# Scanned states by group, slot and part: a change of layout in a two-layer encoder trunk

## The chip, the core and the metric

The kernel runs on one core of one Trainium2 chip. A core has five engines that run their own instruction streams and meet at semaphores: TensorE (PE, with its weight loads PEld), VectorE (DVE), ScalarE (ACT), GpSimd (POOL) and SyncE (SP), which mostly issues transfers (DMA). On-chip memory is SBUF, with 128 partitions, and PSUM, which PE writes. The metric is the time of one execution on the device, in microseconds (us), lower being better.

## The reference

The program is a trunk of two layers over 256 tokens of width 2048. Layer 0 is attention, and the change does not touch it. Layer 1 is a state-space layer: the input projection gives u and a gate z; u is cut into 128 groups of 16 channels, and every group drives 64 complex states in two directions of time.

```python
    bu_re = jnp.einsum('sbgc,gpc->sbgp', u, bb_re)
    bu_im = jnp.einsum('sbgc,gpc->sbgp', u, bb_im)
    ...
    _, _, s_re, s_im = lax.associative_scan(_ssm_combine, (a_re, a_im, bu_re, bu_im), reverse=reverse, axis=0)
    return jnp.einsum('gcp,sbgp->sbgc', c_re, s_re) - jnp.einsum('gcp,sbgp->sbgc', c_im, s_im)
```

In words: the state at each token is the state of the token before, multiplied by a complex number per group and state, plus an input; the output is the real part of a product with c. Forward and backward outputs are summed, a skip and a GELU follow, then a GLU product with a 2048 x 2048 matrix, the gate silu(z), the output projection, a residual sum and a layer norm.

## The kernel before

**Weights.** All large products are made in three passes of rounded operands. A weight chunk of 512 KB is loaded by SP (`raw`, L157, four buffers), rounded on ACT (`wh`, L146, 1024 elements a partition), and its rest is formed on DVE or POOL (`wl`, L148; in the input projection of layer 1 nearly always on POOL). PE then uses both (L210 to L212). Each engine takes its instructions in the order in which the program was built: the kernel's own step loop weaves small tasks of several lanes ("in", "scan", "out", "g", "glu") between the weight chunks, and a wait of one instruction holds up all that stands behind it on its engine.

**The state-space part.** Tokens are taken in chunks of L = 4, so a sequence has NCH = 64 chunks, called slots here. The 128 groups are handled in 16 pieces of PG = 8 groups, and the states of eight pieces (64 groups) are held in one tile V. Partition p of V is a state: 0 to 63 forward, 64 to 127 backward. Along the free axis V holds, per slot, a real and an imaginary part for 64 groups: 64 x 2 x 64 numbers of 4 bytes a partition.

- `in_products` (lane "in"): PE makes the inputs of all slots for one piece (L879) in two PSUM banks `vps`; ACT copies each bank into V (L883), 512 numbers a partition.
- `scan_task` (lane "scan"): 62 steps for each half of 64 groups, all on DVE. A step multiplies the state of slot c - 1 by the coefficients (L896: both products at once into `scp`, which lies in PSUM as the coefficients `cf` do), and adds the two products to slot c (L897 and L898).
- `out_task` (lane "out"): for each piece the scanned states are copied into `su`, ordered by part, group and slot (L918 for the forward partitions, always on ACT; L919 for the backward ones, on ACT for the first eight pieces and on DVE for the last eight, slots in falling order). PE then makes the outputs of the piece (`yps`, L947) from `su`, `om` and `up`, ACT applies GELU (`yg`, L952) and sends the result to HBM, from where `g_task` loads it again and splits it into `gT` (L244 on ACT, L245 on DVE). PSUM has three banks for `vps` and `yps`, so the outputs of a piece must wait until ACT has read those of the third piece before it.

The input projection of the gate (`z`, L1049 and L1051) runs on PE while scan and outputs are under way; the GLU product over `gT` follows, then the output projection.

The coefficient tile is made once, far ahead (L383 to L386), and copied into PSUM when the scan's buffers are opened (L994 and L995).

Of the kernel before, what the change touches and what calls it, by code (L numbers as in the profile page):

```python
# [9 lines left out]
F32 = mybir.dt.float32  # L10
# [3 lines left out]
ALU = mybir.AluOpType  # L14
# [10 lines left out]
G = 128  # L25
# [3 lines left out]
NCH = S // L  # L29
# [3 lines left out]
PG = 8  # L33
# [7 lines left out]
class Trunk:  # L41
# [3 lines left out]
    def __init__(self, ctx, tc, a):  # L45
# [3 lines left out]
        self.s0, self.s1 = self.pool("s0"), self.pool("s1")  # L49
        P = lambda name, bufs, space: ctx.enter_context(tc.tile_pool(name=name, bufs=bufs, space=space))  # L50
        self.dr = P("dr", 1, DRAM)
        self.held, self.tops = ExitStack(), ExitStack()
# [231 lines left out]
    def ssm_tables(self, tp, pp):  # L284

        nc, a, v = self.nc, self.a, self.nc.vector
# [20 lines left out]
        n = T("ex_n")  # L307
# [12 lines left out]
        pw = [None] + [(pws[0][:, k], pws[1][:, k]) for k in range(4)]  # L320
# [48 lines left out]
        f, b = slice(0, 64), slice(64, 128)  # L369
# [10 lines left out]
                            nc.gpsimd.tensor_copy(self.op[i][f, :, c, :, k], src[f])  # L380
                            nc.gpsimd.tensor_copy(self.op[i][b, :, c, :, 3 - k], src[b])

        self.coef = self.const.tile([128, 2, 2, G], F32, name="coef")  # L383
        nc.gpsimd.tensor_copy(self.coef[:, 0], pw[4][0].unsqueeze(1).to_broadcast([128, 2, G]))
        nc.gpsimd.tensor_copy(self.coef[:, 1, 0], pw[4][1])
        v.tensor_scalar(self.coef[:, 1, 1], pw[4][1], -1.0, None, ALU.mult)  # L386

    def ssm_scratch(self):
        d = self.dr
# [476 lines left out]

    def in_products(self, pc, im, up):
        if pc == 8:
            self.V.append(self.s1.tile([128, NCH, 2, 64], F32, tag="s1", name="V"))
        nc, V, g0 = self.nc, self.V[pc // 8], pc % 8 * PG  # L870

        pss = [self.bank("vps").rearrange("p (g r s) -> p g r s", g=4, r=2) for _ in range(2)]
        with self.urgent() if self.IN_URG else ExitStack(), ExitStack() as order:
            for pr in range(4):
                for ri in range(2):
                    for hf, d in ((0, 0), (1, 1), (0, 1), (1, 0)):
                        h = slice(hf * 64, hf * 64 + 64)
                        mv = up[h, 1, pr] if d == 0 else up[h, 0, pr, ::-1]
                        m = nc.tensor.matmul(pss[hf][d * 64:d * 64 + 64, pr, ri], lhsT=im[h, pr, ri, d * 64:d * 64 + 64], rhs=mv, start=True, stop=True)  # L879
                        order.enter_context(self.tc.issue_after(m.ins))  # L880
        with self.urgent():
            for hf in range(2):
                nc.scalar.copy(V[:, :, :, g0 + hf:g0 + PG:2].rearrange("p s r g -> p g r s"), pss[hf])  # L883
        self.flags.add(("V", pc))

    def scan_task(self, p0, p1):

        v = self.nc.vector
        n, g0 = (p1 - p0) * PG, p0 % 8 * PG
        V = self.V[p0 // 8][:, :, :, g0:g0 + n]  # L890
        cf = self.coef[:, :, :, p0 * PG:p1 * PG]
        shp = [128, 2, 2, n]
        for c in range(1, NCH - 1):
            P = self.sc.tile([128, 512], F32, tag="scp", name="scp")[:, :4 * n].rearrange("q (e r g) -> q e r g", e=2, r=2)
            with self.urgent():
                v.tensor_tensor(P, cf, V[:, c - 1].unsqueeze(1).to_broadcast(shp), ALU.mult)  # L896
                v.tensor_tensor(V[:, c], V[:, c], P[:, 0], ALU.add)  # L897
                self.swept = v.tensor_tensor(V[:, c], V[:, c], P[:, 1, ::-1], ALU.add).ins  # L898
            yield
        t = self.now + self.OUT_LAG[p1 == NPIECE]  # L900
        while self.now < t:
            yield
        if p1 == NPIECE:
            self.lanes["out"]["width"] = self.OUT_W2
        for pc in range(p0, p1):
            self.add("out", self.out_task(pc))

    def out_task(self, pc):

        nc, v, wk = self.nc, self.nc.vector, self.wk1  # L910
        b, q = pc // 4, pc % 4
        V = self.V[pc // 8]
        gs = slice(pc % 8 * PG, pc % 8 * PG + PG)
        su = wk.tile([128, 2, PG, NCH], F32, tag="q4", name="su", bufs=self.Q4)
        f, r = slice(0, 64), slice(64, 128)
        nc.gpsimd.memset(su[f, :, :, 0:1], 0.0)
        nc.gpsimd.memset(su[r, :, :, NCH - 1:], 0.0)
        nc.scalar.copy(su[f, :, :, 1:], V[f, 0:NCH - 1, :, gs].rearrange("p s r g -> p r g s"))  # L918
        (v.tensor_copy if pc >= 8 else nc.scalar.copy)(su[r, :, :, :NCH - 1], V[r, NCH - 2::-1, :, gs].rearrange("p s r g -> p r g s"))  # L919
        self.flags.add(("su", pc))  # L920
        tag, bufs = ("im", self.NIM) if self.n_in == NPIECE and self.OMT else ("q4", self.Q4)
        om = wk.tile([128, 2, PG, C * L], F32, tag=tag, name="om", bufs=bufs)
        nc.sync.dma_start(om, self.OMd[pc])
        if pc == 0:
            self.tt = {0: self.turned(0, self.toeplitz(0))}
        if q == 1 and b < NB - 1:
            self.tr = self.toeplitz(b + 1)
        if q == 3 and b < NB - 1:
            self.tt[b + 1] = self.turned(b + 1, self.tr)
        tt = self.tt[b]  # L930
        up = wk.tile([128, 4, NCH], F32, tag="up", name="up2", bufs=3)
        nc.sync.dma_start(up, self.Ud[pc].rearrange("h c t a k -> (h c t) a k"))
        yield
        yield
        ps = self.pm.tile([128, 512], F32, tag="pm", name="yps", bufs=self.npm)

        h = [slice(g % 2 * 64, g % 2 * 64 + 64) for g in range(PG)]
        o = [ps[h[g], g // 2 * NCH:g // 2 * NCH + NCH] for g in range(PG)]
        even, odd = range(0, PG, 2), range(1, PG, 2)
        jobs = [(g, None) for g in even] + [(g, ri) for ri in range(2) for g in range(PG)] + [(g, None) for g in odd]  # L940
        seen = set()
        with ExitStack() as order:
            for n, (g, ri) in enumerate(jobs):
                lhsT = tt[q // 2][h[g], q % 2 * 4 + g // 2].rearrange("q e t -> q (e t)") if ri is None else om[:, ri, g]
                rhs = up[h[g], g // 2] if ri is None else su[:, ri, g]
                stop = ri is None if g % 2 else ri == 1
                m = nc.tensor.matmul(o[g], lhsT=lhsT, rhs=rhs, start=g % 2 not in seen, stop=stop, skip_group_check=True)  # L947
                seen.add(g % 2)
                order.enter_context(self.tc.issue_after(m.ins))
        yield  # L950
        yg = wk.tile([128, 4, NCH], F32, tag="yg", name="yg", bufs=2)
        nc.scalar.activation(yg.rearrange("p a k -> p (a k)"), ps[:, :S], AF.Gelu_apprx_tanh)  # L952
        nc.scalar.dma_start(self.Gd[pc].rearrange("(a h) c t k -> (h c t) a k", h=2), yg)
        self.add("g", self.g_task(pc), *[("su", p) for p in range(8)])
# [32 lines left out]
    def open(self, ssm):  # L987

        self.until(lambda: self.idle("prep"))
        self.prep.close()  # L990
        self.s2 = self.pool("s2", side="right")
        wk = self.wk1 = self.pool("wk1", ssm, side="right")
        self.psum(*self.PSB)
        cf = self.sc.tile([128, 2, 2, G], F32, name="cf")  # L994
        self.nc.scalar.copy(cf, self.coef)  # L995
        self.coef = cf
        self.V = [self.s2.tile([128, NCH, 2, 64], F32, tag="s2", name="V")]
        p0 = 0
        for p1 in self.BATCH:
            self.add("scan", self.scan_task(p0, p1), *[("V", p) for p in range(p0, p1)])  # L1000
            p0 = p1
        self.flags.add("open")
# [207 lines left out]
```

## Time and profile before

| | us |
|---|---|
| median of 3 runs | 894.93 |
| lowest and highest of them | 891.43, 897.63 |
| the profiled execution's own time | 895.47 |
| span of that execution in the trace | 893.7 |

| engine | busy, us | share of the span |
|---|---|---|
| PE | 836.7 | 94% |
| DVE | 654.6 | 73% |
| ACT | 513.9 | 58% |
| POOL | 262.2 | 29% |

The trace covers one execution. Busy time counts instructions of an engine between their start and end; a matmul that runs at a lower granted clock counts as busy for longer, so a busy PE is not a PE at its peak. The share of an engine is a mean over stages: which engine ends a wait has to be read from the stretch in question. Most of layer 1's state-space work lies between 440 and 710 us.

### The profile page before, as it was taken

How to read it: one execution, taken by the hardware profiler on the slowest of the kernel's cores; microseconds unless marked ns; L12 is line 12 of the kernel's file. 1: busy time of each engine (PE TensorE's matmuls, PEld its weight loads, DVE VectorE, ACT ScalarE, POOL GpSimd, SP SyncE). 2: the span in 40 equal slices, each digit the busy share in tenths (PEclk: the TensorE clock that was granted, in tenths of full speed). 3: DMA queues.
4: the chain of work that ended last, by engine and by line, in shares of the span. 5: the costliest groups of instructions: out<-in, count | busy, mean ns of one | idle time of the engine just before them, and what ended most of it. 6: DMA issues, size and time to landing. Idle time of an engine off the chain costs nothing.

```text
span 893.7 us, 18431 instructions
## 1 busy us (share of the span) xinstructions
PE 836.7 (94%) x7244; PEld 759.5 (85%) x7244; DVE 654.6 (73%) x1178; ACT 513.9 (58%) x738; POOL 262.2 (29%) x182
## 2 busy tenths in 40 slices
PE   6999999999999989997999999988997999999992
PEld 4788989889899877886899998987996999988882
DVE  3999889999979968888400598899932459856646
ACT  3554456868677574453565666489749547443321
POOL 0008600000002323333766665843783100000004
PEclk9999999999999999999999999998998899999997
DMA  9765587777676676896789898783996966876723
GB/s 240 237 193 182 140 244 256 208 198 238 166 228 161 199 201 198 244 300 219 254 259 281 252 288 247 224 223 110 276 296 222 269 197 206 237 235 221 241 81 94
DMA packets 217798, 195.82 MB, mean 219 GB/s; under 512 B 67648, under 2 KB 174064, under 8 KB 217456
## 3 DMA queue, kind: packets, MB, share of 16 engines
q1 hardware_dynamic: 200688, 189.93, 71.1%
q10 hardware_dynamic: 17024, 4.72, 2.3%
q8 instruction: 57, 0.93, 0.5%
q14 instruction: 29, 0.24, 0.1%
HBM read 168.39 MB, written 26.21 MB: 218 GB/s over the span
## 4 chain that ended last, share of the span: by engine, by line
PE 62%; DMA 14%; DVE 9%; ACT 5%; issue 5%; SPq 3%; POOL 1%; ACTq 0%; DVEq 0%; POOLq 0%
PE acc L184 10%; PE acc L185 10%; PE acc L186 10%; PE acc L210 8%; PE acc L211 8%; PE acc L212 8%; DMA Ud<-ut 5%; PE yps L947 2%; DMA up<-Ud 1%; PE kps L460 1%; SPq L496 1%; PE vps L879 1%; ACT su L918 1%; DMA raw<-in_w_in_ssm_dram 1%; DMA Gd<-yg 1%
## 5 line engine op out<-in xcount | busy, mean ns | idle before, releaser
L146 ACT CAST wh<-raw 128x1024 fp32r<-128x1024 f32 x234 | 245.1, 1050 | 232.5 <-PE acc L186 76.4
L148 POOL TENSOR_TENSOR wl<-raw,wh 128x1024 fp32r<-128x1024 f32 x84 | 205.9, 2458 | 361.1 <-ACT wh L146 330.9
L148 DVE TENSOR_TENSOR wl<-raw,wh 128x1024 fp32r<-128x1024 f32 x150 | 188.2, 1258 | 49.0 <-ACT wh L146 48.6
L210 PE MATMUL acc<-h1T,wh 128*128 128x256 f32 x512 | 147.2, 292 | 1.9 <-ACT ut L849 1.4
L211 PE MATMUL acc<-h1T,wh 128*128 128x256 f32 x512 | 145.7, 286 | 0.0
L212 PE MATMUL acc<-h1T,wl 128*128 128x256 f32 x512 | 145.0, 284 | 0.0
L896 DVE TENSOR_TENSOR scp<-cf,V 128x256 f32<-128x256 f32 x124 | 53.6, 433 | 72.0 <-ACT V L883 67.8
L210 PEld LDWEIGHTS acc<-h1T,wh 128*128 128x128 f32 x512 | 98.2, 194 | 4.2 <-ACT ut L849 1.6
L211 PEld LDWEIGHTS acc<-h1T,wh 128*128 128x128 f32 x512 | 99.2, 194 | 0.2 <-DVE h1T L844 0.2
L212 PEld LDWEIGHTS acc<-h1T,wl 128*128 128x128 f32 x512 | 99.2, 194 | 0.0
L184 PE MATMUL acc<-wh,xT 128*128 128x512 f32 x192 | 75.6, 399 | 2.5 <-ACT wh L146 2.5
L185 PE MATMUL acc<-wl,xT 128*128 128x512 f32 x192 | 76.0, 396 | 0.8 <-DVE wl L148 0.8
L186 PE MATMUL acc<-wh,xT 128*128 128x512 f32 x192 | 76.1, 396 | 0.0
L212 PE MATMUL acc<-xT,wl 128*128 128x256 f32 x256 | 73.0, 286 | 0.0
L211 PE MATMUL acc<-xT,wh 128*128 128x256 f32 x256 | 72.9, 285 | 0.0
L210 PE MATMUL acc<-xT,wh 128*128 128x256 f32 x256 | 72.7, 284 | 0.0
L210 PE MATMUL acc<-gT,wh 128*128 128x256 f32 x256 | 72.5, 283 | 0.0
L211 PE MATMUL acc<-gT,wh 128*128 128x256 f32 x256 | 71.8, 281 | 0.0
L212 PE MATMUL acc<-gT,wl 128*128 128x256 f32 x256 | 71.7, 280 | 0.0
L1115 POOL TENSOR_TENSOR r<-r,gains 128x512 f32<-128x512 f32 x8 | 11.1, 1410 | 169.9 <-ACT r L1113 169.8
L184 PE MATMUL acc<-wh,oT 128*128 128x512 f32 x128 | 51.3, 408 | 2.8 <-ACT wh L146 2.8
L185 PE MATMUL acc<-wl,oT 128*128 128x512 f32 x128 | 51.0, 400 | 0.0
(257 smaller groups left out, 1898.4 us busy)
## 6 DMA issues: line engine op xcount, KB each, us to landing
raw<-in_w_in_attn_dram SPq DMA_DIRECT2D x80, 512.0 KB, 4.8
raw<-in_w_in_ssm_dram SPq DMA_DIRECT2D x64, 512.0 KB, 6.9
raw<-in_w_out_attn_dram SPq DMA_DIRECT2D x32, 512.0 KB, 5.8
raw<-in_w_glu_dram SPq DMA_DIRECT2D x32, 512.0 KB, 4.7
raw<-in_w_out_ssm_dram SPq DMA_DIRECT2D x32, 512.0 KB, 5.6
IMd<-im SPq DMA_DIRECT2D x16, 512.0 KB, 4.1
OMd<-om SPq DMA_DIRECT2D x16, 512.0 KB, 5.4
im<-IMd SPq DMA_DIRECT2D x16, 512.0 KB, 6.6
```

The source lines that it names most:

```text
L146: nc.scalar.copy(wh, raw)
L148: (nc.gpsimd if i - self.first in range(*self.POOL) or i in self.POOL0 else nc.vector).tensor_tensor(wl, raw, wh.bitcast(F32), ALU.subtract)
L184: nc.tensor.matmul(ps, lhsT=xh, rhs=wh[:, kk], start=kb == 0, stop=False)
L185: nc.tensor.matmul(ps, lhsT=xh, rhs=wl[:, kk], start=False, stop=False)
L186: nc.tensor.matmul(ps, lhsT=xl, rhs=wh[:, kk], start=False, stop=kb == KB - 1)
L210: nc.tensor.matmul(o, lhsT=wh[:, kk, f], rhs=ah[:, kb], start=kb == 0 and not (one and i), stop=False, skip_group_check=one)
L211: nc.tensor.matmul(o, lhsT=wh[:, kk, f], rhs=al[:, kb], start=False, stop=False, skip_group_check=one)
L212: self.mm = nc.tensor.matmul(o, lhsT=wl[:, kk, f], rhs=ah[:, kb], start=False, stop=kb == KB - 1, skip_group_check=one).ins
L460: nc.tensor.matmul(kps[h * 64:h * 64 + 64, pr * 32:pr * 32 + 32], lhsT=X[:, ri, g].rearrange("q c t -> q (c t)"), rhs=cd[:, ri, g].rearran ...
L896: v.tensor_tensor(P, cf, V[:, c - 1].unsqueeze(1).to_broadcast(shp), ALU.mult)
L947: m = nc.tensor.matmul(o[g], lhsT=lhsT, rhs=rhs, start=g % 2 not in seen, stop=stop, skip_group_check=True)
L1115: (nc.gpsimd if k == "g" else v).tensor_tensor(x, x, o, op)
```

## The change

V, the product tile P, and the coefficients are laid out by group, slot and part instead of slot, part and group. The real and the imaginary number of one group and slot become neighbours; the slots of one group follow each other at 8 bytes; the groups lie 64 x 2 x 4 = 512 bytes apart. Before, the 64 groups of one slot and part were neighbours, and the slots lay 2 x 64 x 4 = 512 bytes apart. Sizes, buffers, values and the order of the sums are the same.

```diff
-        self.coef = self.const.tile([128, 2, 2, G], F32, name="coef")
-        nc.gpsimd.tensor_copy(self.coef[:, 0], pw[4][0].unsqueeze(1).to_broadcast([128, 2, G]))
-        nc.gpsimd.tensor_copy(self.coef[:, 1, 0], pw[4][1])
-        v.tensor_scalar(self.coef[:, 1, 1], pw[4][1], -1.0, None, ALU.mult)
+        self.coef = self.const.tile([128, 2, G, 2], F32, name="coef")
+        nc.gpsimd.tensor_copy(self.coef[:, 0], pw[4][0].unsqueeze(2).to_broadcast([128, G, 2]))
+        nc.gpsimd.tensor_copy(self.coef[:, 1, :, 0], pw[4][1])
+        v.tensor_scalar(self.coef[:, 1, :, 1], pw[4][1], -1.0, None, ALU.mult)
...
-            self.V.append(self.s1.tile([128, NCH, 2, 64], F32, tag="s1", name="V"))
+            self.V.append(self.s1.tile([128, 64, NCH, 2], F32, tag="s1", name="V"))
...
-                nc.scalar.copy(V[:, :, :, g0 + hf:g0 + PG:2].rearrange("p s r g -> p g r s"), pss[hf])
+                nc.scalar.copy(V[:, g0 + hf:g0 + PG:2].rearrange("p g s r -> p g r s"), pss[hf])
...
-        V = self.V[p0 // 8][:, :, :, g0:g0 + n]
-        cf = self.coef[:, :, :, p0 * PG:p1 * PG]
-        shp = [128, 2, 2, n]
+        V = self.V[p0 // 8][:, g0:g0 + n]
+        cf = self.coef[:, :, p0 * PG:p1 * PG]
+        shp = [128, 2, n, 2]
         for c in range(1, NCH - 1):
-            P = self.sc.tile([128, 512], F32, tag="scp", name="scp")[:, :4 * n].rearrange("q (e r g) -> q e r g", e=2, r=2)
+            P = self.sc.tile([128, 512], F32, tag="scp", name="scp")[:, :4 * n].rearrange("q (e g r) -> q e g r", e=2, r=2)
             with self.urgent():
-                v.tensor_tensor(P, cf, V[:, c - 1].unsqueeze(1).to_broadcast(shp), ALU.mult)
-                v.tensor_tensor(V[:, c], V[:, c], P[:, 0], ALU.add)
-                self.swept = v.tensor_tensor(V[:, c], V[:, c], P[:, 1, ::-1], ALU.add).ins
+                v.tensor_tensor(P, cf, V[:, :, c - 1].unsqueeze(1).to_broadcast(shp), ALU.mult)
+                v.tensor_tensor(V[:, :, c], V[:, :, c], P[:, 0], ALU.add)
+                self.swept = v.tensor_tensor(V[:, :, c], V[:, :, c], P[:, 1, :, ::-1], ALU.add).ins
...
-        nc.scalar.copy(su[f, :, :, 1:], V[f, 0:NCH - 1, :, gs].rearrange("p s r g -> p r g s"))
-        (v.tensor_copy if pc >= 8 else nc.scalar.copy)(su[r, :, :, :NCH - 1], V[r, NCH - 2::-1, :, gs].rearrange("p s r g -> p r g s"))
+        nc.scalar.copy(su[f, :, :, 1:], V[f, gs, 0:NCH - 1].rearrange("p g s r -> p r g s"))
+        (v.tensor_copy if pc >= 8 else nc.scalar.copy)(su[r, :, :, :NCH - 1], V[r, gs, NCH - 2::-1].rearrange("p g s r -> p r g s"))
...
-        cf = self.sc.tile([128, 2, 2, G], F32, name="cf")
+        cf = self.sc.tile([128, 2, G, 2], F32, name="cf")
```

The instructions of all five engines stay in the same order and in the same number. Only the forms of the scan's two sums differ. On DVE the end of the layer norm's splits and the start of the scan read so before (names are as above; h1T and ht belong to the layer norm):

```order
L844 TENSOR_TENSOR h1T<-ht,h1T 128x256
L896 TENSOR_TENSOR scp<-cf,V 128x256
L897 TENSOR_TENSOR V<-V,scp 128x128
L898 TENSOR_TENSOR V<-V,scp 128x128
L896 TENSOR_TENSOR scp<-cf,V 128x256
```

And now:

```order
L844 TENSOR_TENSOR h1T<-ht,h1T 128x256
L896 TENSOR_TENSOR scp<-cf,V 128x256
L897 TENSOR_TENSOR V<-V,scp 128x64x2
L898 TENSOR_TENSOR V<-V,scp 128x64x2
L896 TENSOR_TENSOR scp<-cf,V 128x256
```

Nothing moved; the two sums go over 64 pairs instead of one run of 128. On ACT the copies into `su` of the fourth and fifth piece, with the weight cast, the z copy and the GELU among them, read the same before and now:

```order
L918 COPY su<-V 64x16x63
L919 COPY su<-V 64x16x63
L146 CAST wh<-raw 128x1024
L1051 COPY z_6637<-acc_7437 128x256
L918 COPY su<-V 64x16x63
L919 COPY su<-V 64x16x63
L952 ACT_TABLE_LOAD
L952 ACTIVATE yg<-yps 128x256
```

Their shape (2 x 8 rows of 63 slots) is unchanged too; what changes is the distance between two slots in V.

## Rows read from the trace of the kernel before

**Rows 1.** Busy time by stretch: length, busy time of each engine, granted clock, DMA.

```profile
core 0: us, PE busy (x) PEld busy (x) DVE busy (x) ACT busy (x) POOL busy (x), PEclk, DMA share, GB/s
...
592.00:628.00 36.00, 29.46 (x327) 28.08 (x326) 32.68 (x97) 35.25 (x27) 13.61 (x11) 0.91 0.53 152
628.00:668.00 40.00, 39.57 (x446) 37.59 (x445) 27.41 (x45) 24.39 (x33) 29.13 (x22) 1.00 0.95 289
668.00:700.00 32.00, 25.84 (x362) 23.84 (x362) 6.94 (x8) 25.61 (x24) 11.55 (x12) 0.79 0.73 226
```

**Rows 2.** Waits of PE, 430 to 720 us: total us, times, longest.

```profile
PE yps L947 <- ACT yg L952: 7.3, 2, 4.0
PE yps L947 <- ACT su L918: 2.9, 1, 2.9
PE yps L947 <- ACT su L919: 2.5, 2, 2.1
...
PE vps L879 <- ACT V L883: 1.1, 1, 1.1
```

**Rows 3.** Timeline of PE: start, length, instruction, idle time before and its releaser.

```profile
600.40 1.15 PE L947 MATMUL yps<-su,om 128*64 128x64 f32 x32 [2.14 <-ACT su L919]
...
615.30 0.68 PE L947 MATMUL yps<-up,tt 64*64 64x64 f32 x8 [4.00 <-ACT yg L952]
...
673.90 1.64 PE L947 MATMUL yps<-su,om 128*64 128x64 f32 x32 [2.88 <-ACT su L918]
...
689.45 1.11 PE L947 MATMUL yps<-up,tt 64*64 64x64 f32 x8 [3.29 <-ACT yg L952]
```

**Rows 4.** Timeline of ACT in the same stretches.

```profile
592.36 2.06 ACT L918 COPY su<-V 64x1008 f32<-64x1008 f32 x1
...
614.87 0.38 ACT L952 ACTIVATE yg<-yps 128x256 f32<-128x256 f32 x1
...
671.94 7.47 ACT L918 COPY su<-V 64x1008 f32<-64x1008 f32 x4
...
689.02 0.38 ACT L952 ACTIVATE yg<-yps 128x256 f32<-128x256 f32 x1
```

**Rows 5.** Groups of ACT by form: busy us, mean ns, idle before and releasers.

```profile
L146 ACT CAST wh<-raw 128x1024 fp32r<-128x1024 f32 x234 | 245.1, 1050 | 232.5 <-PE acc L186 76.4 <-PE acc L211 74.4 <-issue 24.0
L883 ACT COPY V<-vps 128x512 f32<-128x512 f32 x32 | 32.4, 1120 | 8.8 <-PE vps L879 5.1 <-ACT ut L849 3.0 <-DMA up<-Ud 0.7
L918 ACT COPY su<-V 64x1008 f32<-64x1008 f32 x16 | 31.2, 1968 | 0.1
...
L453 ACT COPY im<-imps 128x512 f32<-128x512 f32 x32 | 17.6, 590 | 8.6 <-PE imps L442 6.0 <-DMA IMd<-im 2.5
...
L919 ACT COPY su<-V 64x1008 f32<-64x1008 f32 x8 | 15.8, 1971 | 0.1
```

**Rows 6.** Instructions on V: ns least/median/most, first and last start.

```profile
L896 DVE TENSOR_TENSOR scp<-cf,V x124: 432/433/433, 500.5 to 639.8; 128x256 f32<-128x256 f32 x124
...
L898 DVE TENSOR_TENSOR V<-V,scp x124: 286/288/291, 501.3 to 640.6; 128x128 f32<-128x128 f32 x124
...
L919 DVE COPY su<-V x8: 1298/1358/3551, 652.8 to 685.7; 64x1008 f32<-64x1008 f32 x8
```

**Rows 7.** Groups of DVE by form, two of 1024 elements.

```profile
L148 DVE TENSOR_TENSOR wl<-raw,wh 128x1024 fp32r<-128x1024 f32 x150 | 188.2, 1258 | 49.0 <-ACT wh L146 48.6
...
L421 DVE TENSOR_TENSOR X<-B,xp 128x1024 f32<-128x1024 f32 x16 | 19.5, 1220 | 6.4 <-DMA B<-in_b_im_dram 4.4 <-PE kps L460 2.0
```

**Rows 8.** Instructions on the coefficient tile.

```profile
L386 DVE TENSOR_SCALAR coef<-pw x1: 700/700/700, 88.8 to 88.8; 128x128 f32<-128x128 f32 x1
...
L995 ACT COPY cf<-coef x1: 591/591/591, 438.7 to 438.7; 128x512 f32<-128x512 f32 x1
```

**Rows 9.** Timeline of DVE where the scan ends.

```profile
640.57 0.29 DVE L898 TENSOR_TENSOR V<-V,scp 128x128 f32<-128x128 f32 x1
640.77 7.16 DVE L245 TENSOR_TENSOR gT<-gp,gT 128x256 fp32r<-128x256 f32 x4
...
652.85 6.13 DVE L919 COPY su<-V 64x1008 f32<-64x1008 f32 x3
```

More of the change, by code (lines that the diff above doesn't have):

```diff
@@ L993, in open @@
         self.psum(*self.PSB)
-        cf = self.sc.tile([128, 2, 2, G], F32, name="cf")
+        cf = self.sc.tile([128, 2, G, 2], F32, name="cf")
         self.nc.scalar.copy(cf, self.coef)
         self.coef = cf
-        self.V = [self.s2.tile([128, NCH, 2, 64], F32, tag="s2", name="V")]
+        self.V = [self.s2.tile([128, 64, NCH, 2], F32, tag="s2", name="V")]
         p0 = 0
```

## The prediction, made before the change was run

> **What bounds the kernel now.** I read the profile in this order: busy time by stretch, the waits of the matrix engine (PE), its timeline at those waits, the timeline of ScalarE (ACT) at the same moments, and last the durations of the instructions that touch V and su, beside rows of equal size without a stride.
>
> Over most of the layer PE simply works. There are two holes [rows 1]. From 592 to 628 us PE is busy for 29.46 of 36 us at a mean granted clock of 0.91; from 668 to 700 us for 25.84 of 32 us at 0.79. In between, 39.57 of 40 us are busy at 1.00. In work at full clock the holes lose 36 − 29.46 × 0.91 = 9.2 us and 32 − 25.84 × 0.79 = 11.6 us, so 20.8 us is all that can be won there. In the first hole ACT is busy for 35.25 of 36 us: it is the engine that sets the pace.
>
> The waits say the same [rows 2]: PE waits for ACT's yg (7.3 us, twice) and for the su copies (2.9 and 2.5 us). In the timeline [rows 3] the wait before 615.30 (4.00 us, on yg) and the one before 600.40 (2.14 us, on su) lie in the first hole, those before 673.90 (2.88 us, su) and 689.45 (3.29 us, yg) in the second. The yg that PE needs is a small instruction (0.38 us at 614.87), and PE is late for it because ACT stands in its queue behind su copies [rows 4]: from 592.36 on come eight of some 2 us each, then a weight cast, a z copy, two more su copies and a table load. In the second hole four su copies run from 671.94 (7.47 us) and two more before the yg at 689.02.
>
> So what matters is what one su copy costs. It takes 1968 ns on ACT for 1008 elements a partition, while a copy of 512 elements without a stride takes 590 ns and a cast of 1024 takes 1050 ns [rows 5]. The slope of the latter two is (1050 − 590) / 512 = 0.898 ns an element, so 1008 elements would cost 590 + 496 × 0.898 = 1036 ns. The copy of V out of PSUM, 512 elements written with a stride, takes 1120 ns, where 590 is the price without one. Both walk V in steps of 512 bytes: the inner index is the slot, and 128 words lie between slots. The hopping costs (1968 − 1036) / 1008 = 0.925 ns an element.
>
> **The change, part by part.** It adds, removes and moves no instruction on any engine or queue, so no wait changes its partner and no transfer its place. It changes three access patterns.
>
> 1. *The su copies on ACT* (24 of them, L918 sixteen times and L919 eight times). Between neighbouring slots now lie 8 bytes instead of 512. Bounds: 1036 ns (no price for a step of two words) and 1968 ns (the same price as now). I take 1.04 us, since a step of two words is nearer to adjacent words than to 512 bytes. That frees 0.93 us a copy, 22 us of ACT in all.
>    First hole: ten su copies stand ahead of the yg at 614.87, so it comes 9.3 us earlier, near 605.6. [...] Of the 9.2 us I count 8.
>    Second hole: one copy stands between the last weight cast and 673.90, worth 0.9 us. Six stand between 671.94 and 689.02, worth 5.6 us, more than the 3.29 us of wait. The clock took 25.84 × 0.21 = 5.4 us; I count 1 of it, since the wait at 673.90 stays for 2 us and lowers the clock as before. Together 5.
> 2. *The copies into V on ACT* (32, L883). 1120 becomes 590 ns, bounds 590 and 1120; 17 us of ACT. PE waited for them for 1.1 us in all [rows 2], and in that stretch ACT has room, so I count 0.5.
> 3. *The scan on VectorE (DVE)*: 124 steps of one product of 256 and two sums of 128 elements, 433 and 288 ns, from 500.5 to 640.9 us, so 140.4 / 124 = 1.13 us a step with all gaps [rows 6]. What was a contiguous run of 128 words in V is now 64 pairs of words, 512 bytes apart. No row shows pairs. Bounds: nothing, or ACT's 0.925 ns on every element read from V, (256 + 128) × 0.925 = 0.36 us a step. I take nothing: each second element still lies beside the first, and L421, whose second operand jumps back after every fourth word, takes 1220 ns, no more than the 1258 ns of L148, which has the same size and no jump [rows 7]. The writes and the swapped halves of P in PSUM are treated the same. Nothing is forecast below zero: no operand of the scan gets a longer run than it had.
>
>    The eight su copies on DVE (L919, 1298 ns at the least [rows 6]) keep their price in the sum; they lie beside PE's work. The coefficients are written with a stride once, at 88.8 us, for 0.7 us, and are first read at 438.7 us [rows 8]: even at several times the price nothing waits.
>
> [...] The rows show 0.925 ns for an element that lies 512 bytes from the last one, and none shows 8 bytes. [...]
>
> The sum: 8 + 5 + 0.5 = 13.5 us. The profiled execution took 895.47 us (span 893.7), half a microsecond above the median of 894.93. 895.5 − 13.5 = **882 us**. What is late next is the transfers: between the holes they already take 0.95 of their engines' time [rows 1]. After 700 us nothing is touched, and the rest shifts as a whole.
>
> **Rivals.**
> - *The step of 8 bytes costs what 512 bytes cost.* For it speaks that su and V cost about the same per element though one reads and the other writes, as if any non-adjacent word paid. Against it, that no row has a short step. Then ACT frees nothing: **895**, between 892 and 898. Chance 0.13.
> - *The first hole closes and the second does not.* PE would reach the second hole 8 us early, with transfers at 0.95 in between; weights, om and yg's way through memory then hold it where ACT did. 895.5 − 8 = **888**. For it: 0.95 [rows 1]. Against: in the first hole the transfer engines are busy for 0.53 only, so the weights can come earlier. Chance 0.12.
> - *The scan becomes the bound, and the kernel slower.* If the pairs pay on each word read, a step grows by 0.36 us, 124 steps by 44 us, and the scan ends at 685 instead of 641. Then come four gT sums (7.2 us) and the first su copy of the second half (6.13 / 3 = 2.0 us) [rows 9]: done near 694, where PE wants it at 673.9 [rows 3]. PE is held for 20 us, the gain of the first hole is lost in that wait, and some 3 us of the second hole's waits vanish: **912**. Its point of decision: DVE needs 9.2 us after the scan, so it holds PE beyond today's 673.9 only when the scan ends after 664.7, 23.8 us later, that is at 0.19 us a step or more. Chance 0.11.
>
> **How the numbers follow.** My case has 0.64; its own range is 875 to 889, as the clock may give back more (all of 20.8 would be 875) or the second hole nothing but its first wait. Predicted is 882. The range of 8 in 10 takes in the second rival and most of the first: 874 to 897, and leaves out the third (0.11) and some 0.06 at the edges. One per cent is 9 us, about what a measurement of this kernel can tell from no change (three runs lay between 891.43 and 897.63). Faster by over 1% means below 886.0: 0.52 of my 0.64 and 0.02 from the second rival, 0.54. Slower by over 1%: the third rival, 0.11. Within 1%: 0.35.
>
> **What would show it.** L918 at about 1.04 us and L883 at 0.59 us: step right; either near its old price: first rival. L896 at 433 and L897/L898 at 288 ns, the scan ending near 640: step 3 right; a step above 1.3 us: third rival. PE's wait for yg near 615 gone and the granted clock between 592 and 628 back at 1.00: the first hole is closed. The wait for yg in the second hole gone but PE waiting for raw or om instead: second rival. I am wrong in size if ACT is as fast as said and PE's idle time in the two holes falls by less than half.

## The result and the profile after

The changed kernel took 879.52 us (median of 4 runs, 874.92 to 884.24) beside 893.18 us for the kernel before (median of 4): ratio 0.9846, 95% interval 0.9802 to 0.989. Of 893.18 us that is a gain of 13.8 us (9.8 to 17.7). A second set of runs (e5 below) gave 877.75 beside 892.99 us, ratio 0.983, 0.98 to 0.9861. The profiled execution took 879.38 us, 877.6 of them in the span, 16.1 less than before.

First the prices. Groups of ACT by form (busy us, mean ns), which answer to [rows 5]:

```profile
L883 ACT COPY V<-vps 128x512 f32<-128x512 f32 x32 | 18.3, 633 | 9.6 <-ACT ut L849 5.4 <-PE vps L879 3.4 <-PE acc L212 0.7
L918 ACT COPY su<-V 64x1008 f32<-64x1008 f32 x16 | 17.9, 1135 | 1.2 <-PE yps L947 1.1
...
L919 ACT COPY su<-V 64x1008 f32<-64x1008 f32 x8 | 9.2, 1152 | 0.1
```

And the instructions of DVE on V (least/median/most ns, first and last start), beside [rows 6]:

```profile
L896 DVE TENSOR_TENSOR scp<-cf,V x124: 432/432/433, 499.0 to 637.2; 128x256 f32<-128x256 f32 x124
...
L898 DVE TENSOR_TENSOR V<-V,scp x124: 288/290/300, 499.8 to 638.0; 128x128 f32<-128x128 f32 x124
...
L919 DVE COPY su<-V x8: 679/684/724, 642.3 to 677.2; 64x1008 f32<-64x1008 f32 x8
```

A su copy on ACT fell from 1968 to 1135 ns, a copy into V from 1120 to 633, and a su copy on DVE from 1298 (the least) to 679. The medians of the scan's three instructions stayed within 2 ns. Now the stretches, beside [rows 1]:

```profile
592.00:628.00 36.00, 35.48 (x457) 33.66 (x456) 32.68 (x97) 31.92 (x36) 18.14 (x18) 1.00 0.71 207
628.00:668.00 40.00, 37.08 (x410) 35.15 (x410) 18.21 (x42) 22.55 (x34) 27.84 (x21) 0.94 0.97 302
668.00:700.00 32.00, 32.00 (x418) 30.49 (x416) 9.73 (x12) 20.02 (x27) 6.10 (x6) 0.91 0.84 264
```

The first hole is closed: PE is busy for 35.48 of 36 us, at full clock. The second hole now lies some 11 us earlier. Finer stretches around it:

```profile
652.00:664.00 12.00, 9.93 (x108) 9.46 (x107) 1.28 (x3) 6.92 (x8) 10.31 (x8) 0.98 0.96 316
664.00:676.00 12.00, 12.00 (x124) 11.21 (x124) 2.67 (x5) 11.79 (x14) 1.50 (x5) 0.59 0.68 224
```

PE stands idle for 2.07 us and then works through 12 us at a mean granted clock of 0.59 (0.50 of full speed from 664 to 672 us, 1.00 from 674 to 676); 12 × 0.41 = 4.9 us of work are lost there. Waits of PE from 430 to 720 us, beside [rows 2]:

```profile
PE yps L947 <- ACT su L918: 2.1, 1, 2.1
...
PE yps L947 <- ACT su L919: 0.5, 1, 0.5
PE vps L879 <- ACT V L883: 0.5, 1, 0.5
```

No wait for yg is left; the two su waits that remain are these in PE's timeline, beside [rows 3]:

```profile
596.38 1.15 PE L947 MATMUL yps<-su,om 128*64 128x64 f32 x32 [0.52 <-ACT su L919]
...
662.46 1.15 PE L947 MATMUL yps<-su,om 128*64 128x64 f32 x32 [2.07 <-ACT su L918]
```

On ACT, beside [rows 4], the first yg came at 605.90 instead of 614.87, and the one at 689.02 now at 673.46:

```profile
591.68 1.13 ACT L918 COPY su<-V 64x1008 f32<-64x1008 f32 x1
...
605.90 0.39 ACT L952 ACTIVATE yg<-yps 128x256 f32<-128x256 f32 x1
...
661.30 4.21 ACT L918 COPY su<-V 64x1008 f32<-64x1008 f32 x4
...
673.46 0.38 ACT L952 ACTIVATE yg<-yps 128x256 f32<-128x256 f32 x1
```

Where the time came from is read from one group that runs in both kernels, the products of `up` and `tt` (first and last start). Before:

```profile
L947 PE MATMUL yps<-up,tt x256: 218/218/366, 586.5 to 705.5; 64*64 64x64 f32 x128
```

After:

```profile
L947 PE MATMUL yps<-up,tt x256: 218/218/366, 584.6 to 689.6; 64*64 64x64 f32 x128
```

PE enters the first hole 1.9 us earlier. The output of the ninth piece, which waits for its su copy in both, starts at 662.46 instead of 673.90, 11.4 us earlier: the first hole gave 9.5. The last output ends the second hole 15.9 us earlier: that one gave 4.5. The rest of the kernel shifted as a whole, to 16.1 us at the end. These shifts belong to one trace of each kernel; by the medians the gain is 13.8 us.

### The profile page after: what moved, and what is told of

The parts are those of the page before. It is cut to its first block, busy times and chain, and to the rows that moved or that the text cites. A ratio compares the mean times of both kernels' runs of the same rounds, so it can differ in the third digit from the quotient of the medians.

```text
span 877.6 us, 18431 instructions
## 1 busy us (share of the span) xinstructions
PE 831.8 (95%) x7244; PEld 756.4 (86%) x7244; DVE 644.6 (73%) x1178; ACT 480.2 (55%) x738; POOL 259.0 (30%) x182
## 4 chain that ended last, share of the span: by engine, by line
PE 64%; DMA 15%; DVE 11%; ACT 4%; issue 3%; SPq 3%; POOL 1%; ACTq 0%; DVEq 0%; POOLq 0%
PE acc L184 9%; PE acc L185 9%; PE acc L186 9%; PE acc L210 9%; PE acc L211 8%; PE acc L212 8%; DMA Ud<-ut 4%; PE yps L947 2%; DVE wl L148 2%; DMA raw<-in_w_in_ssm_dram 2%; DMA Gd<-yg 2%; PE kps L460 1%; DMA up<-Ud 1%; SPq L496 1%; PE vps L879 1%
## 5 line engine op out<-in xcount | busy, mean ns | idle before, releaser
L896 DVE TENSOR_TENSOR scp<-cf,V 128x256 f32<-128x256 f32 x124 | 53.6, 432 | 68.3 <-ACT V L883 64.1
```

What stands on the lines that cost most here:

```text
L896: v.tensor_tensor(P, cf, V[:, :, c - 1].unsqueeze(1).to_broadcast(shp), ALU.mult)
```

## The experiments

Two theories stood against each other: that the shorter su copies on ACT carry the gain, and that the copies into V, or the scan on pairs, carry it. Beside that, three prices were open: that of a step of 8 bytes, that of single words in the scan, and that of what is left of the second hole. All ratios are to the kernel before, run on the same chip.

| run | us, median | ratio | 95% interval |
|---|---|---|---|
| e1, su copies hop 512 bytes again | 894.5 | 1.0005 | 0.9981 to 1.003 |
| e2, copies into V slow again | 879.87 | 0.9829 | 0.9794 to 0.9864 |
| e3, slot innermost | 914.43 | 1.0226 | 1.018 to 1.0272 |
| e4, su copies of the second half on DVE | 873.99 | 0.9773 | 0.9736 to 0.981 |
| e5, the changed kernel again | 877.75 | 0.983 | 0.98 to 0.9861 |
| e6, e4 again, beside e5 | 875.47 | 0.9786 | 0.9754 to 0.9819 |
| e7, old layout with the DVE copies of e4 | 882.77 | 0.9879 | 0.9845 to 0.9914 |
| e8, steps of 16 and 32 bytes | 905.37 | one run | |

**e1: the su copies undone.**

```diff
-        nc.scalar.copy(su[f, :, :, 1:], V[f, gs, 0:NCH - 1].rearrange("p g s r -> p r g s"))
...
+        nc.scalar.copy(su[f, :, :, 1:], V[f, 0:NCH - 1, NCH - 9:NCH - 1].rearrange("p s g r -> p r g s"))
+        (v.tensor_copy if pc >= 8 else nc.scalar.copy)(su[r, :, :, :NCH - 1], V[r, NCH - 2::-1, NCH - 9:NCH - 1].rearrange("p s g r -> p r g s"))
```

> The changed kernel, with one part undone: the copies into su (L918, L919) walk V in steps of 512 bytes again, with as many elements and the same waits; what they copy is not what the outputs need. V copies and scan stay as changed. My theory, that the su copies on ACT carry nearly the whole gain: L918 back near 1.97 us, both holes open again, only the 1.9 us that PE was ahead at the first hole stay: 889 to 893 us, ratio to the kernel before 0.995 to 1.000. Rival, that the shorter copies into V or the scan in pairs carry it: the time stays near 880 us, ratio 0.985.

Instructions on V, the two holes, and the longest waits of PE from 430 to 720 us:

```profile
L883 ACT COPY V<-vps x32: 618/626/647, 452.9 to 555.3; 128x512 f32<-128x512 f32 x32
L918 ACT COPY su<-V x16: 1892/1958/2123, 589.6 to 690.1; 64x1008 f32<-64x1008 f32 x16
```

```profile
592.00:628.00 36.00, 29.90 (x313) 27.98 (x311) 32.67 (x98) 35.15 (x27) 11.84 (x12) 0.86 0.52 147
...
668.00:700.00 32.00, 27.37 (x371) 25.26 (x370) 6.81 (x8) 25.03 (x24) 10.73 (x11) 0.79 0.69 219
```

```profile
PE yps L947 <- ACT yg L952: 3.1, 3, 1.5
PE yps L947 <- ACT su L918: 2.9, 1, 2.9
PE yps L947 <- ACT su L919: 2.7, 2, 2.1
```

Both holes are as large as before, though the copies into V are fast and the scan goes over pairs. The whole gain is gone: the su copies carry it. The edit also slows the eight su copies on DVE (1297 ns at the least), but these waits of PE are all for ACT, and e7 below gains with copies on DVE at their old price (1320 ns at the least). The lead that I had left to the copies into V does not show in the ratio, which lies just above the range expected; the interval reaches down to 0.9981, so some 1.7 us of it are not excluded.

**e2: the copies into V undone.**

```diff
-                nc.scalar.copy(V[:, g0 + hf:g0 + PG:2].rearrange("p g s r -> p g r s"), pss[hf])
+                nc.scalar.copy(V[:, g0 + hf:g0 + PG:2].rearrange("p g s r -> p r s g"), pss[hf].rearrange("p g r s -> p r s g"))
```

> The changed kernel, with the other part undone: the copies into V (L883) go over the same numbers in an order whose neighbours lie 1 KB apart in V and 512 bytes apart in PSUM, so that they are slow again (1.1 us or more instead of 0.63). The su copies and the scan stay. My theory: it costs the 1.9 us that PE gained ahead of the first hole, 881 to 883 us, ratio 0.986 to 0.989. Rival, that the copies into V carry the gain: back to 891 to 895 us, ratio near 1.000.

```profile
L883 ACT COPY V<-vps x32: 1060/1140/1196, 456.1 to 559.0; 128x512 f32<-128x512 f32 x32
```

At 1140 ns, as slow as before, they cost nothing that can be measured: 0.9829 beside 0.9846 and 0.983. The expected 1.9 us did not come, and the second theory, that these copies carry the gain, falls. That the lead with which PE enters the first hole is worth nothing is not shown, though. The interval is some 3 us wide to either side. And in e2's trace PE enters the first hole 2.4 us later than in the changed kernel (the first output starts at 587.0 instead of 584.6) is still 3.0 us behind at the ninth piece (665.47 and 662.46), and is level with it at the last output (689.5 and 689.6): in between, the stretch at the lower clock was shorter in e2, as the lines in the last section show. So that trace hides the lead in something else.

**e3: slot innermost.** The order is group, part, slot.

```diff
...
-                v.tensor_tensor(P, cf, V[:, :, c - 1].unsqueeze(1).to_broadcast(shp), ALU.mult)
-                v.tensor_tensor(V[:, :, c], V[:, :, c], P[:, 0], ALU.add)
...
+                v.tensor_tensor(P, cf, V[:, :, :, c - 1].unsqueeze(1).to_broadcast(shp), ALU.mult)
+                v.tensor_tensor(V[:, :, :, c], V[:, :, :, c], P[:, 0], ALU.add)
...
-        self.V = [self.s2.tile([128, 64, NCH, 2], F32, tag="s2", name="V")]
+        self.V = [self.s2.tile([128, 64, 2, NCH], F32, tag="s2", name="V")]
```

> Layout by group, part and slot: the copies into V and su read and write words in a row (step 4 bytes instead of 8), and the scan's operands in V are single words 256 bytes apart instead of pairs. [...] Rival, that only the step from word to word counts and is not priced at 8 bytes by halves: L918 falls to 1.04 us. Rival, that DVE's sums hide the hops: a step stays at 1.12 us and the ratio is 0.983.

```profile
L896 DVE TENSOR_TENSOR scp<-cf,V x124: 583/620/649, 503.0 to 698.3; 128x256 f32<-128x256 f32 x124
L897 DVE TENSOR_TENSOR V<-V,scp x124: 410/436/458, 503.6 to 698.9; 128x128 f32<-128x128 f32 x124
L898 DVE TENSOR_TENSOR V<-V,scp x124: 410/436/455, 504.1 to 699.3; 128x128 f32<-128x128 f32 x124
L883 ACT COPY V<-vps x32: 581/591/615, 457.7 to 560.4; 128x512 f32<-128x512 f32 x32
L918 ACT COPY su<-V x16: 1017/1033/1043, 620.5 to 714.4; 64x1008 f32<-64x1008 f32 x16
...
L919 DVE COPY su<-V x8: 678/684/727, 701.4 to 714.5; 64x1008 f32<-64x1008 f32 x8
```

Waits in PE's timeline:

```profile
622.64 1.97 PE L947 MATMUL yps<-su,om 128*64 128x64 f32 x32 [24.34 <-ACT su L919]
...
702.23 1.97 PE L947 MATMUL yps<-su,om 128*64 128x64 f32 x32 [10.75 <-ACT su L918]
```

Single words cost a scan step (620 − 432) + (436 − 289) + (436 − 290) = 481 ns, twice the 0.24 us that come of the price that the su copies on DVE lost, (1298 − 679) / 1008 = 0.61 ns, on 256 + 128 words, and more than the 0.36 us that the prediction had set as its upper bound; over 124 steps that is 60 us, and the scan ends at 699.6 us. It holds PE in both holes, and the kernel is slower than before: the ratio is 1.0226, where I had set 1.015 as the most. The copies on ACT gain a little: 1033 ns at a step of 4 bytes beside 1130 at 8, which is 0.096 ns an element; on DVE nothing (684 beside 684). Here I missed as well: I had expected L918 to stay at the 1.13 us of 8 bytes, and it fell to the 1.04 us of the rival.

**e4 and e6: the second half's su copies on DVE.**

```diff
-        nc.scalar.copy(su[f, :, :, 1:], V[f, gs, 0:NCH - 1].rearrange("p g s r -> p r g s"))
+        (v.tensor_copy if pc >= 8 else nc.scalar.copy)(su[f, :, :, 1:], V[f, gs, 0:NCH - 1].rearrange("p g s r -> p r g s"))
```

> The changed kernel, with both su copies of the last eight pieces on DVE (0.68 us each there), L918 too. If what is left of the second hole is PE's wait for L918 behind a weight cast on ACT (2.07 us at 662.46) and the lower clock after it (664 to 676 us at 0.59, 4.9 us): 873 to 876 us, ratio 0.977 to 0.981. Rival: the program's order on PE, which moves the outputs of these pieces later by some matmuls, brings yg and gT later and the GLU product waits for them: 880 us or more, ratio 0.985 and above.

> The changed kernel itself, beside e6 on the same chip: 878 to 882 us, ratio to the kernel before 0.981 to 0.988.

> The kernel of e4 again, to set it beside the changed kernel on one chip. If the gain of e4 is real: 872 to 876 us, 4 to 8 us below e5. If it was the spread of the runs: the two within 2 us.

The stretches of e6:

```profile
592.00:628.00 36.00, 35.26 (x455) 33.36 (x454) 32.68 (x98) 31.09 (x36) 18.37 (x18) 1.00 0.72 213
628.00:668.00 40.00, 37.35 (x380) 35.63 (x379) 23.19 (x42) 22.49 (x31) 28.70 (x18) 0.96 0.90 282
668.00:700.00 32.00, 32.00 (x471) 30.38 (x470) 17.95 (x19) 13.49 (x23) 7.95 (x10) 1.00 0.96 313
```

Twice this version had the lowest median: 873.99 and 875.47 us, both as expected. The changed kernel beside it came at 877.75 us, just under the range set for e5. On one chip the version of e6 is thus 2.3 us lower, less than the 4 to 8 expected; the two intervals just overlap, so that it beats the changed kernel is likely and not settled. Against the kernel before it wins (1 − 0.9786) × 892.99 = 19.1 us, near all of the 20.8 us that the two holes held. The wait for L918 is gone, but another stands in its place in e6, as the timelines of PE and ACT show:

```profile
661.40 0.39 PE L210 MATMUL acc<-gT,wh 128*128 128x256 f32 x1 [2.26 <-ACT z L1051]
```

```profile
660.03 1.04 ACT L146 CAST wh<-raw 128x1024 fp32r<-128x1024 f32 x1 [2.75 <-DMA raw<-in_w_glu_dram]
660.98 0.36 ACT L1051 COPY z<-acc 128x256 f32<-128x256 f32 x1
```

PE now waits for a z copy that stands on ACT behind a weight cast, and that cast waited for its transfer. What e6 has over the changed kernel is most of the slow stretch after the wait. The rival, that outputs placed later on PE would hold up the GLU product, did not come true.

**e7: the old layout with the copies of e4.** The same edit in the kernel before.

> The layout of before, with both su copies of the last eight pieces on DVE (1.3 us each there). The first hole is untouched, since its copies stay on ACT at 1.97 us; the second loses the eight L918 on ACT. My theory, that the two holes are worth 9 and 5 us on their own: 4 to 7 us below the kernel before, 888 to 891 us, ratio 0.992 to 0.996. Rival, that what ACT is freed of in the second hole has no worth as long as the first is open: ratio 0.998 to 1.002.

```profile
592.00:628.00 36.00, 30.58 (x319) 28.79 (x318) 32.66 (x98) 35.23 (x28) 12.24 (x11) 0.86 0.52 148
...
668.00:700.00 32.00, 30.66 (x451) 28.84 (x449) 22.36 (x17) 15.76 (x23) 21.65 (x13) 1.00 0.92 298
```

The first hole stays, the second closes, and (1 − 0.9879) × 892.99 = 10.8 us come of it: more than the 4 to 7 that I expected, and near the 11.6 us counted in the prediction. So the second hole alone is worth 10.8 us when ACT is freed of all eight copies, and the changed kernel, which only shortens them, takes 4.5 of it. If the two holes simply add, what e6 has beyond e7 is the first: 19.1 − 10.8 = 8.3 us. The rival, that the second hole has no worth while the first is open, fell.

**e8: steps of 16 and 32 bytes.**

```diff
...
+        nc.scalar.copy(su[f].rearrange("p r g (t s) -> p r g t s", t=2), V[f, gs].rearrange("p g (s t) r -> p r g t s", t=2))
+        by4, by2 = V[r, gs].rearrange("p g (s t) r -> p r g t s", t=4), V[r, gs].rearrange("p g (s t) r -> p r g t s", t=2)
...
+            nc.scalar.copy(su[r].rearrange("p r g (t s) -> p r g t s", t=4), by4)
...
```

> One look at prices: the su copies go over all 64 slots in another order, L918 on ACT by steps of 16 bytes, L919 on ACT by 32 bytes, and on DVE by 32 bytes in odd pieces and 16 bytes in even ones (1024 elements instead of 1008; the order of slots in su is not what the outputs need). [...] If the price grows with the distance: 16 bytes between 1.13 and 1.97 us, 32 bytes above it. If small steps that are not adjacent are dearer than large ones: above 2.1 us on ACT, and above 1.3 us on DVE.

The rows in order: ACT by 16 bytes, ACT by 32, DVE by 16, DVE by 32.

```profile
L918 ACT COPY su<-V x16: 2004/2060/2114, 589.6 to 693.0; 64x1024 f32<-64x1024 f32 x16
L921 ACT COPY su<-V x8: 2041/2090/2177, 591.7 to 637.1; 64x1024 f32<-64x1024 f32 x8
L925 DVE COPY su<-V x4: 1074/1081/1156, 651.7 to 682.6; 64x1024 f32<-64x1024 f32 x4
L923 DVE COPY su<-V x4: 1095/1102/1171, 652.8 to 693.5; 64x1024 f32<-64x1024 f32 x4
```

On ACT the whole price is paid at 16 bytes: 2060 / 1024 = 2.01 ns an element, where 512 bytes cost 1968 / 1008 = 1.95, 8 bytes 1.13 and 4 bytes 1.02. The cliff on ACT lies between 8 and 16 bytes, and beyond it distance hardly matters (2.01 ns at 16 bytes, 2.04 at 32, 1.95 at 512). On DVE 16 and 32 bytes cost 1.06 and 1.08 ns, between the 0.68 at 8 and the 1.29 at 512 bytes. So the price of 512 bytes holds on ACT at 16 and at 32 bytes, and on DVE it does not. The price that grows with the distance does not show on ACT beyond 16 bytes, and no median passed 2.1 us on ACT or 1.3 us on DVE. Steps of 16 and 32 bytes are cheaper than 512 on DVE, and 3 to 5% dearer on ACT. These copies also go over shorter rows, of 32 and 16 slots instead of 63, in an order of one dimension more. The length of the rows can carry little of the price on ACT, as rows of 32 and of 16 cost nearly the same (2060 and 2090 ns); the further dimension was not tried by itself. The program's order differs a little in this kernel, as other slots are waited for, and 905.37 us is one run; its time is not used.

## Why the prediction was right

1. *The su copies on ACT, forecast 1.04 us and 13 us of gain.* The mechanism was right, shown by e1 (take it back, and nothing is left) and e2. The price came out at 1135 ns: a step of two words is not quite free on ACT (at 4 bytes it was 1033 ns, in e3). The rows that it was bounded by were the right ones, and the choice between them, an estimate, as no row had a step of 8 bytes, held: 8 bytes lie on the near side of the cliff that e8 found on ACT. Steps of 4 bytes go at 1.02 ns an element, of 8 bytes at 1.13, of 16 bytes at 2.01; what in the chip makes that cliff no run shows. On DVE the scan's pairs kept the price of a run of words (290 ns beside 288), and the su copies cost 684 ns at 8 and at 4 bytes.
2. *The first hole, forecast 8 us.* No run shows the term of 8 us as it was put together, from waits and clock; for the whole hole the runs showed 9.5 us by the outputs' starts and 8.3 by e6 less e7. The first yg came 9.0 us earlier (605.90 for 614.87; forecast 605.6), before PE wanted it.
3. *The second hole, forecast 5 us.* 4.5. The wait for yg went, the wait for the first L918 shrank from 2.88 to 2.07 us and the lower clock followed it, all as said. Of the clock's loss almost nothing came back, where 1 us was counted: 25.84 × 0.21 = 5.4 us before, 37.08 × 0.06 + 32 × 0.09 = 5.1 us after. What I did not see is how much lay there: e7 takes 10.8 us out of it.
4. *The copies into V, forecast 0.5 us.* They became short (633 ns, forecast 590), and PE came to the first hole 1.9 us earlier. Neither that lead nor what it is worth is settled: with the short copies the first output starts between 583.5 us (e6) and 587.4 (e4), with the long ones between 585.3 (e7) and 587.0 (e2), and by e1 and e2 no gain shows at the end within the intervals.
5. *The scan, forecast unchanged.* 432 and 290 ns. That the reasoning was needed shows e3: single words cost 60 us. My bound of 0.36 us a step (44 us in all) was too low, and the sum itself was wrong: a step reads 256 elements of V in the product and 128 in each of the two sums, and I counted one sum. With both it is 512 × 0.925 = 0.47 us, 59 us in all, beside 0.48 and 60 measured. The parts agree less well: the product pays 188 / 256 = 0.73 ns an element and a sum 147 / 128 = 1.15, which would fit if a word that is written pays as well, but no run shows that by itself. And I looked for the damage in the second hole only, where e3 shows 24 us of wait in the first.
6. *The su copies on DVE, forecast unchanged.* Wrong: they halved. The step that failed is that they keep their price; 679 ns came of 1298. It cost nothing in the sum, as no wait of PE is for them. The move to DVE in e4 does not hang on it, as it pays in e7 at the old price too.

The sum of 13.5 us met 13.8 (9.8 to 17.7), and 882 met 879.5 us. That the two sums are so close is in part luck: the interval is 8 us wide, the first hole gave up to 1.5 us more than its term and the second 0.5 less, and the term of the copies into V is not shown. The first rival fell by the price of L918, the third by L896. The second fell by PE's waits, where no transfer of weights appears, though much of the second hole stayed open: 2.07 us of wait and 4.9 us of clock.

## What to carry to other kernels

When an operand is walked in two ways, look for an order that gives one way steps of 8 bytes and the other pairs of adjacent words, as here: pairs, though 512 bytes apart, kept the scan at its price (a sum took 290 ns beside 288) and brought the copies on ACT near theirs (1135 ns beside 1968 before and 1033 at 4 bytes), while the order with single words for the scan (e3) ruined it (481 ns more a step, ratio 1.0226). Find the engine that a waiting PE stands behind, and look at the price per element of what fills that engine's queue, not at its share of the span. And ask first whether another engine stands idle there: moving the copies of one half to DVE gave the old layout 10.8 us without any change of layout.

## What the runs showed of the hardware that I had not expected

A one-source copy on DVE goes at 0.68 ns an element with a step of 4 or 8 bytes (684 ns for 1008 elements in e3 and in the changed kernel), beside 1.29 at 512 bytes. The layout halved these copies and left the scan's sums alone, which went from one run of words to pairs (288 and 290 ns).

PE's lower clock does not follow from the length of a wait alone. Stretches after the wait in the second hole, in the changed kernel (2.07 us of wait) and in e5, the same kernel again (2.09 us):

```profile
664.00:674.00 10.00, 10.00 (x104) 9.41 (x103) 2.67 (x5) 9.94 (x13) 1.50 (x5) 0.51 0.81 267
```

```profile
663.00:673.00 10.00, 10.00 (x104) 9.40 (x103) 3.11 (x5) 9.94 (x12) 2.17 (x7) 0.50 0.91 299
```

The same in e2 (2.08 us of wait) and in e6 (2.26 us, with products of the GLU behind it instead of outputs):

```profile
666.00:670.00 4.00, 4.00 (x67) 3.70 (x64) 0.68 (x2) 4.00 (x7) 1.74 (x4) 0.57 0.73 243
670.00:680.00 10.00, 10.00 (x173) 9.32 (x172) 2.85 (x5) 9.94 (x11) 2.64 (x7) 1.00 0.78 261
```

```profile
662.00:666.00 4.00, 4.00 (x24) 4.00 (x23) 0.76 (x2) 3.63 (x5) 1.54 (x1) 0.58 0.66 226
666.00:676.00 10.00, 10.00 (x188) 9.19 (x187) 5.19 (x7) 4.26 (x6) 5.98 (x8) 1.00 0.72 227
```

After waits of nearly one length (2.07 to 2.26 us) PE ran for some 10 us at a granted clock of 0.51 and 0.50 in two traces, and for less than 4 us at a lowered one in two others (0.57 and 0.58 over the 4 us above, 1.00 behind them). What decides between them stays open, and so does how much of the spread of some 9 us between runs of one kernel comes of it.
